# Windowed attention on one core: the first loads issued by GpSimd at once, and the last store split between two queues

## The chip, the cores and the metric

The kernel runs on one core of a Trainium2 chip. The metric is the device time in microseconds (us); the time before is the median of five runs.

## The reference

Attention inside windows of 64 rows, over 4 batches of 4096 rows of 1536 float32 numbers. Every window is on its own.

```
B, S, D = q.shape                      # 4, 4096, 1536, float32
W = 64
q_w = q.reshape(B, S // W, W, D)       # k_w, v_w alike
logits = einsum('bnwd,bnud->bnwu', q_w, k_w) * D ** -0.5
attn = exp(logits - logits.max(-1)) ; attn = attn / attn.sum(-1)
out = einsum('bnwu,bnud->bnwd', attn, v_w)
```

Inputs are three tensors of 100.7 MB each in float32, the output is one more.

## The kernel before, in words

The 16,384 rows are cut into 32 units of 512 rows (UR = 128 x 4 slots; N = 32). For one unit, q, k and v are each 3.15 MB of float32 in HBM and half of that in SBUF, because GpSimd's loads cast to float16 in flight (`load`, line 106). A unit goes through these steps:

- **Transposes** (line 145): TensorE transposes q and k in blocks, two float16 numbers packed as one float32. VectorE and ScalarE copy the results out of PSUM by turns (line 220) into `xq` and `xk`.
- **Products** (line 157): TensorE multiplies the transposed q and k; ScalarE takes the exponential of the four 32x128 blocks that a window pair needs (line 262).
- **Sums and outputs** (line 113): TensorE multiplies by a column of ones for the sums and by v for the outputs. VectorE and ScalarE scale them (lines 249 and 273) into one of three float32 buffers, `outs`.

Loads land in two buffers for each of q, k and v. `hand_over` on GpSimd waits for a landing, waits until the working tile is free, copies it there (line 294), tells TensorE, and requests the load of the unit two ahead into the emptied buffer. So from the start on some six loads and one or two stores are queued in GpSimd's DMA queue, in one fixed order written out by hand: q, k, store of the unit before, v. `store` issues a unit's output as one transfer (line 279). Loads and stores from GpSimd run in one DMA queue, those from SyncE in another; both feed the same 16 DMA engines.

Two places lie outside this pattern.

**The start** (lines 304 to 328). The first q does not come through GpSimd. SyncE loads it as float32 into `outs[0]` in four pieces: two halves of slot 0, slot 1, slots 2 and 3, each with its own semaphore (`d_r0` to `d_r3`). GpSimd waits for the first piece, makes the identity matrix (`affine_select`, line 315), issues the first k and v, and then casts the four slots one by one into `q16` (line 324), waiting for the pieces; between and after the casts it requests the loads of units 1 and 2. SyncE, after its four issues, waits for the identity, the memsets, the four casts, the first k and the first v (lines 353 to 358), and passes these on to TensorE.

**The end** (lines 373 to 390). The last unit's output is stored in two halves, both by SyncE (line 377): the first when each of VectorE and ScalarE has written its first output of the second half, the second when each has written its last. GpSimd drains and raises `done`; SyncE waits for `done` and for all stores (line 387), and clears the semaphores.

Of the kernel before, what the change touches and what calls it, by code (L numbers as in the profile page):

```python
# [17 lines left out]
def kernel(  # L18
# [13 lines left out]
    nc = tc.nc  # L32
    PE, DVE, ACT = (getattr(mybir.EngineType, e) for e in ("PE", "DVE", "Activation"))
    B, S, D = q.shape
    DC = D // (2 * P)
    NJ = D // 512
    SLOTS, R, H = 4, 2, 2
# [3 lines left out]
    qf, kf, vf, of = (x.rearrange("b s d -> (b s) d") for x in (q, k, v, out))  # L41

    def sb(name, shape, dtype):
        return ctx.enter_context(nc.sbuf_tensor(name, shape, dtype))
# [6 lines left out]
    def sem(name):  # L51
        sems.append(nc.alloc_semaphore(name))
        return sems[-1]

    q16 = sb("q16", [P, SLOTS, D], FP16)
    k16 = sb("k16", [P, SLOTS, D], FP16)
# [6 lines left out]
    outs = [sb(f"out{i}", [P, SLOTS, D], FP32) for i in range(NO)]  # L63
# [7 lines left out]
    ops = [ps(f"o{j}", [P, 512]) for j in range(NJ)]  # L71
    sp = ps("sp", [P, 4])

    d_r0, d_r1, d_r2, d_r3, d_k0, d_v0 = (
        sem(n) for n in ("d_r0", "d_r1", "d_r2", "d_r3", "d_k0", "d_v0")
    )
    landed = {x: [sem(f"d_{x}{i + 1}") for i in range(NL)] for x in "qkv"}
    d_o = [sem(f"d_o{i}") for i in range(NO)]
    d_l = [sem(f"d_l{i}") for i in range(2)]
    g_q, g_k, g_v = (sem(n) for n in ("g_q", "g_k", "g_v"))  # L80
# [10 lines left out]
    n_e = [sem("n_ed"), sem("n_ea")]  # L91
    i_d, i_p, c_q, c_l, done = (sem(n) for n in ("i_d", "i_p", "c_q", "c_l", "done"))
# [4 lines left out]
    def rows(x, row0, n, r):  # L97
        return x[row0 : row0 + P * n].rearrange("(h p r) d -> p h (r d)", p=P, r=r)

    def slots(t, lo, hi, r):  # L100
        return t[:, lo:hi, :].rearrange("p (h r) d -> p h (r d)", r=r)

    def load(name, u, dst, s):
        src = {"q": qf, "k": kf, "v": vf}[name]
        r = R if name == "v" else SLOTS
        nc.gpsimd.dma_start(
            out=slots(dst, 0, SLOTS, r), in_=rows(src, u * UR, SLOTS, r)
        ).then_inc(s, 16)
# [169 lines left out]
    def store(u):  # L278
        nc.gpsimd.dma_start(
            out=rows(of, u * UR, SLOTS, R), in_=slots(outs[u % NO], 0, SLOTS, R)  # L280
        ).then_inc(d_o[u % NO], 16)

    def request(x, u):
        if u < N:
            load(x, u, landing[x][u % NL], landed[x][u % NL])
# [3 lines left out]
    def hand_over(x, u, dst, m, g):  # L289

        gp = nc.gpsimd
        gp.wait_ge(landed[x][u % NL], 16 * ((u + u % NL) // NL))
        gp.wait_ge(m, u)
        gp.tensor_copy(  # L294
            out=dst[:, :, :].bitcast(FP32), in_=landing[x][u % NL][:, :, :].bitcast(FP32)
        ).then_inc(c_l, 1)
        copies[0] += 1
        gp.wait_ge(c_l, copies[0])
        gp.sem_inc(g, 1)
        request(x, u + NL)  # L300

    with tc.tile_critical(no_gpsimd_drain=True):

        raw = rows(qf, 0, SLOTS, SLOTS).rearrange("p h (r d) -> p (h r) d", d=D)
        for lo, hi, c0, c1, s in (
            (0, 1, 0, D // 2, d_r0), (0, 1, D // 2, D, d_r1), (1, 2, 0, D, d_r2), (2, SLOTS, 0, D, d_r3)
        ):
            nc.sync.dma_start(
                out=outs[0][:, lo:hi, c0:c1], in_=raw[:, lo:hi, c0:c1]
            ).then_inc(s, 16)  # L310
        nc.vector.memset(ident[:, :], 0.0).then_inc(i_d, 1)
        nc.gpsimd.wait_ge(i_d, 1)

        nc.gpsimd.wait_ge(d_r0, 16)
        nc.gpsimd.affine_select(
            out=ident[:, :], in_=ident[:, :], compare_op=mybir.AluOpType.not_equal,
            fill=1.0, base=0, pattern=[[-1, P]], channel_multiplier=1,
        ).then_inc(i_p, 1)
        load("k", 0, k16, d_k0)
        load("v", 0, v16, d_v0)  # L320

        for i in range(SLOTS):
            nc.gpsimd.wait_ge((d_r1, d_r2, d_r3, d_r3)[i], 16)
            nc.gpsimd.tensor_copy(out=q16[:, i, :], in_=outs[0][:, i, :]).then_inc(c_q, 1)
            if i == 1:
                request("q", 1)
        for x, u in (("k", 1), ("v", 1), ("q", 2), ("k", 2), ("v", 2)):
            request(x, u)

        nc.vector.memset(ones[:, :], 1.0).then_inc(i_d, 1)  # L330
        nc.vector.memset(zeros[:, :], 0.0).then_inc(i_d, 1)
        for et in ets:
            nc.vector.memset(et[:, :, :, :], 0.0).then_inc(i_d, 1)
        nc.scalar.wait_ge(i_d, 5)
        nc.scalar.activation(zeros[:, 3:4], zeros[:, 0:1], EXP, bias=zeros[:, 0:1], scale=1.0)

        with nc.Fori(0, N, engines=OrderedEngineSet([PE]), head_slot={PE: 0}):
            tensor_unit()
        assert N % NO == 2
        for eng, unit in ((DVE, vector_unit), (ACT, scalar_unit)):  # L340
            with nc.Fori(0, N // NO, engines=OrderedEngineSet([eng]), head_slot={eng: 0}):
                for u in range(NO):
                    unit(u)
            for u in range(N - 2, N):
                unit(u)

        sy = nc.sync
        for j in range(NJ):
            for n in (2, 3):
                sy.sem_inc(f_o[j][n], 1)  # L350
        for a in range(2):
            sy.sem_inc(fr[a], NO)
        sy.wait_ge(i_p, 1)
        sy.wait_ge(i_d, 5)
        sy.wait_ge(c_q, SLOTS)
        sy.sem_inc(g_q, 1)
        sy.sem_inc(g_k, 1)._wait_ge(d_k0, 16)
        sy.sem_inc(g_v, 1)._wait_ge(d_v0, 16)
        for u in range(NO, N):
            sy.wait_ge(d_o[u % NO], 16 * (u // NO))  # L360
            for a in range(2):
                sy.sem_inc(fr[a], 1)

        gp = nc.gpsimd
        for u in range(1, N):
            hand_over("q", u, q16, m_q, g_q)
            hand_over("k", u, k16, m_k, g_k)
            gp.wait_ge(m_q, u + 1)
            store(u - 1)
            hand_over("v", u, v16, m_v, g_v)  # L370


        base, o = (N - 1) * UR, outs[(N - 1) % NO]
        for h, c in enumerate((1, 3)):
            for a in range(2):
                sy.wait_ge(n_e[a], c)
            sy.dma_start(
                out=rows(of, base + R * P * h, R, R), in_=slots(o, R * h, R * h + R, R)
            ).then_inc(d_l[h], 16)
        gp.drain()  # L380
        gp.sem_inc(done, 1)
        sy.wait_ge(done, 1)
        for i in range(NO):
            last = max(u for u in range(N - 1) if u % NO == i)
            sy.wait_ge(d_o[i], 16 * (last // NO + 1))
        for i in range(2):
            sy.wait_ge(d_l[i], 16)
        lo, hi = min(s.num for s in sems), max(s.num for s in sems)
        assert hi - lo + 1 == len(sems)
        sy.sem_clear(range(lo, hi + 1))  # L390


# [28 lines left out]
```

## Time and profile before

| what | value |
|---|---|
| median of 5 runs | 942.98 us (942.55 to 943.0) |
| profiled execution, its own time | 942.71 us |
| its span, first to last instruction | 940.9 us |
| its mean granted TensorE clock | 0.857 |
| TensorE busy | 659.4 us (70%) |
| GpSimd busy | 340.4 us (36%) |
| HBM traffic | 301.99 MB read, 100.66 MB written |
| from issue to landing, first k and first v | 12.8 us, 19.4 us |
| from issue to landing, the two last halves (median) | 9.6 us |

The span is the time between the first and the last instruction of one profiled execution; the execution's own time has 1.81 us more around it. In the lines of the profile, "POOL" is GpSimd, "SP" is SyncE, "DVE" VectorE, "ACT" ScalarE and "PE" TensorE. "L106" is line 106 of the kernel; the line of a helper stands for all its calls, so the tile names tell them apart (`q` is q16, `ql` a landing buffer, `out` one of `outs`). A row of the order of time gives start, duration, engine, line, operation, and in brackets the idle time before it with what ended it. A row of the stretches gives the window, its length, the busy time and count of each engine, the granted clock, the mean busy share of the 16 DMA engines and the GB/s they moved, counted on the SBUF side. That share can pass 1, since a transfer's packet is counted whole where it starts. HBM traffic counts float32 bytes, so a cast load counts twice its SBUF bytes there.

### The profile page before, as it was taken

The numbers are of one execution on the slowest core, as the hardware profiler recorded it, in microseconds if no ns is written. First come the engines' busy times: TensorE is split into PE (matmuls) and PEld (weight loads), VectorE is DVE, ScalarE is ACT, GpSimd is POOL, SyncE is SP. The second block draws the span as 40 slices with busy tenths as digits, with TensorE's granted clock in tenths as the row PEclk, the third lists the DMA queues.
The fourth block names the chain that finished last, engine by engine and source line by source line (L and its number), as shares of the span: only waits on it lengthen the run. The fifth ranks groups of instructions, "written<-read, shape, count | busy, mean of one in ns | idle before, by whom it ended". The sixth has DMA issues, their size and how long they took to land. (4 is left out here: it accounts for less than half of the span.)

```text
span 940.9 us, 11422 instructions
## 1 busy us (share of the span) xinstructions
PE 659.4 (70%) x4096; PEld 399.4 (42%) x3456; DVE 279.6 (30%) x453; ACT 335.9 (36%) x642; POOL 340.4 (36%) x228
## 2 busy tenths in 40 slices
PE   1888676866867767677677676776867767677672
PEld 1555344533445334444344543444433355344440
DVE  0433321333313333133332233322333223332231
ACT  1444433333333333332433324333333333343332
POOL 4344333344333443333423334233343333433221
PEclk9999988889888888887988778978888888888887
DMA  9999999999999999999999999999999999999998
GB/s 254 218 215 280 258 243 282 282 282 265 236 281 282 282 275 234 274 282 281 280 235 269 283 280 282 242 261 281 282 282 249 253 281 282 281 258 245 281 300 363
DMA packets 27084, 253.35 MB, mean 269 GB/s; under 512 B 2112, under 2 KB 2112, under 8 KB 10688
## 3 DMA queue, kind: packets, MB, share of 16 engines
q0 software_dynamic: 26208, 246.95, 100.0%
q1 hardware_dynamic: 864, 6.29, 1.7%
q14 instruction: 10, 0.08, 0.0%
q8 instruction: 2, 0.03, 0.0%
HBM read 301.99 MB, written 100.66 MB: 428 GB/s over the span
## 5 line engine op out<-in xcount | busy, mean ns | idle before, releaser
L157 PE MATMUL lt<-xq,xk 128*128 128x256 f16 x1536 | 217.5, 294 | 0.0
L145 PE MATMUL tp<-ident,k 128*128 128x128 f32 x768 | 149.8, 340 | 84.5 <-PEq L211 74.8
L294 POOL COPY v<-vl 128x3072 f32<-128x3072 f32 x31 | 85.2, 2747 | 295.9 <-DMA vl<-in_v_dram 295.9
L157 PEld LDWEIGHTS lt<-xq,xk 128*128 128x128 f16 x1536 | 160.6, 105 | 34.0
L145 PE MATMUL tp<-ident,q 128*128 128x128 f32 x768 | 113.1, 295 | 70.6 <-DVE xq L220 35.3
L145 PEld LDWEIGHTS tp<-ident,k 128*128 128x128 f32 x768 | 115.9, 177 | 104.4 <-issue 101.8
L220 ACT COPY xk<-tp 128x512 f32<-128x512 f32 x96 | 59.5, 620 | 266.1 <-ACTq L211 266.1
L186 PEld LDWEIGHTS <-et 128*128 128x128 f16 x384 | 34.4, 107 | 277.5 <-issue 271.6
L145 PEld LDWEIGHTS tp<-ident,q 128*128 128x128 f32 x768 | 91.8, 151 | 111.4 <-issue 110.8
L220 DVE COPY xk<-tp 128x512 f32<-128x512 f32 x96 | 66.5, 693 | 231.8 <-DVEq L211 231.8
L294 POOL COPY q<-ql 128x3072 f32<-128x3072 f32 x31 | 85.0, 2742 | 110.0 <-DMA ql<-in_q_dram 110.0
L294 POOL COPY k<-kl 128x3072 f32<-128x3072 f32 x31 | 85.2, 2747 | 107.9 <-DMA kl<-in_k_dram 107.9
L113 PE MATMUL o<-v,et 128*128 128x512 f16 x384 | 113.1, 439 | 0.0
L262 ACT ACTIVATE et<-lt,zeros 32x128 f16<-32x128 f32 x256 | 92.1, 360 | 39.4 <-ACTq L211 36.2
L113 PE MATMUL sp<-ones,et 128*128 128x1 f16 x256 | 25.6, 169 | 113.1 <-PEq L211 110.8
L220 ACT COPY xq<-tp 128x512 f32<-128x512 f32 x96 | 59.9, 624 | 125.0 <-ACTq L211 125.0
L249 DVE TENSOR_SCALAR out<-o,rs 128x512 f32<-128x512 f32 x128 | 91.0, 747 | 32.5 <-DVEq L211 28.3
L220 DVE COPY xq<-tp 128x512 f32<-128x512 f32 x96 | 66.3, 690 | 92.6 <-DVEq L211 92.3
L273 ACT ACTIVATE out<-tp,rs 128x512 f32<-128x512 f32 x64 | 44.0, 688 | 135.5 <-ACTq L211 105.0
L113 PE MATMUL tp<-v,et 128*128 128x512 f16 x256 | 91.0, 442 | 0.0
L239 DVE RECIPROCAL rs<-sp 128x2 f32<-128x2 f32 x64 | 10.7, 168 | 260.7 <-DVEq L211 260.6
L113 PE MATMUL lt<-v,et 128*128 128x512 f16 x128 | 57.5, 449 | 0.0
(21 smaller groups left out, 224.0 us busy)
## 6 DMA issues: line engine op xcount, KB each, us to landing
out_dram<-out POOLq DMA_DIRECT2D x31, 3072.0 KB, 61.8
ql<-in_q_dram POOLq DMA_DIRECT2D x31, 1536.0 KB, 54.9
kl<-in_k_dram POOLq DMA_DIRECT2D x31, 1536.0 KB, 54.9
vl<-in_v_dram POOLq DMA_DIRECT2D x31, 1536.0 KB, 54.9
out_dram<-out SPq DMA_DIRECT2D x2, 1536.0 KB, 9.6
out<-in_q_dram SPq DMA_DIRECT2D x1, 1536.0 KB, 13.2
k<-in_k_dram POOLq DMA_DIRECT2D x1, 1536.0 KB, 12.8
v<-in_v_dram POOLq DMA_DIRECT2D x1, 1536.0 KB, 19.4
```

Source lines behind the costliest of these rows:

```text
L113: return nc.tensor.add_instruction(mybir.InstMatmult(name=nc.get_next_instruction_name(), engine=PE, ins=[low(rhs), low(w)], outs=[low(o)] ...
L145: ins = nc.tensor.transpose(tps[g % 2][:, r, j, :], pairs[:, c * P : (c + 1) * P], ident[:, :])
L157: ins = nc.tensor.matmul(lts[h][:, r, :, :], lhsT=halves(xk, c)[:, r, h, :, w], rhs=halves(xq, c)[:, :, h, :, w], start=(c == 0 and w == 0 ...
L186: ld = nc.tensor.ldweights(w)
L220: copy(out=dst, in_=tps[g % 2][:, :, :, :]).then_inc(f_c[g % 4], 1)
L239: ve.reciprocal(out=rs[:, n : n + R], in_=sp[:, n : n + R]).then_inc(n_d, 1)
L249: ins = ve.tensor_scalar_mul(scaled(u, n, j), bank(n, j), scalar1=rs[:, n : n + 1])
L262: ins = sc.activation(ets[h][s, :, :, s], lts[h][s, :, :, s], EXP, bias=zeros[s, 0:1], scale=scale)
L273: ins = sc.activation(scaled(u, n, j), bank(n, j), COPY, bias=0.0, scale=rs[:, n : n + 1])
L294: gp.tensor_copy(out=dst[:, :, :].bitcast(FP32), in_=landing[x][u % NL][:, :, :].bitcast(FP32)).then_inc(c_l, 1)
```

## The change

It has two parts.

- **The start.** SyncE loads only slot 0 of the first q as float32, in one transfer of 0.79 MB, on `d_r0`. GpSimd loads slots 1 to 3 itself, cast to float16, straight into `q16` (a new semaphore, `d_q0`), then the first k; then it makes the identity as soon as the memset is done, loads the first v, and requests all of units 1 and 2. Only then does it wait for `d_r0` and cast the one slot. The other three waits and casts are gone. SyncE waits for one cast and for `d_q0`.
- **The end.** The first half of the last store is issued by GpSimd, the second still by SyncE; each engine waits for the outputs itself. SyncE waits for all stores and raises `done`; GpSimd waits for that and clears the semaphores.

```diff
-        raw = rows(qf, 0, SLOTS, SLOTS).rearrange("p h (r d) -> p (h r) d", d=D)
-        for lo, hi, c0, c1, s in (
-            (0, 1, 0, D // 2, d_r0), (0, 1, D // 2, D, d_r1), (1, 2, 0, D, d_r2), (2, SLOTS, 0, D, d_r3)
-        ):
-            nc.sync.dma_start(
-                out=outs[0][:, lo:hi, c0:c1], in_=raw[:, lo:hi, c0:c1]
-            ).then_inc(s, 16)
+        first = rows(qf, 0, SLOTS, SLOTS)
+        nc.sync.dma_start(out=outs[0][:, 0, :], in_=first[:, 0, :D]).then_inc(d_r0, 16)
+        nc.gpsimd.dma_start(
+            out=q16[:, 1:, :].rearrange("p r d -> p (r d)"), in_=first[:, 0, D:]
+        ).then_inc(d_q0, 16)
+        load("k", 0, k16, d_k0)
         nc.vector.memset(ident[:, :], 0.0).then_inc(i_d, 1)
         nc.gpsimd.wait_ge(i_d, 1)
-
-        nc.gpsimd.wait_ge(d_r0, 16)
         nc.gpsimd.affine_select(
...
-        load("k", 0, k16, d_k0)
         load("v", 0, v16, d_v0)
-
-        for i in range(SLOTS):
-            nc.gpsimd.wait_ge((d_r1, d_r2, d_r3, d_r3)[i], 16)
-            nc.gpsimd.tensor_copy(out=q16[:, i, :], in_=outs[0][:, i, :]).then_inc(c_q, 1)
-            if i == 1:
-                request("q", 1)
-        for x, u in (("k", 1), ("v", 1), ("q", 2), ("k", 2), ("v", 2)):
-            request(x, u)
+        for u in (1, 2):
+            for x in "qkv":
+                request(x, u)
+        nc.gpsimd.wait_ge(d_r0, 16)
+        nc.gpsimd.tensor_copy(out=q16[:, 0, :], in_=outs[0][:, 0, :]).then_inc(c_q, 1)
...
-        sy.wait_ge(c_q, SLOTS)
-        sy.sem_inc(g_q, 1)
+        sy.wait_ge(c_q, 1)
+        sy.sem_inc(g_q, 1)._wait_ge(d_q0, 16)
...
-        for h, c in enumerate((1, 3)):
+        for h, (eng, c) in enumerate(((gp, 1), (sy, 3))):
             for a in range(2):
-                sy.wait_ge(n_e[a], c)
-            sy.dma_start(
+                eng.wait_ge(n_e[a], c)
+            eng.dma_start(
...
         gp.drain()
-        gp.sem_inc(done, 1)
-        sy.wait_ge(done, 1)
         for i in range(NO):
...
+        sy.sem_inc(done, 1)
+        gp.wait_ge(done, 1)
...
-        sy.sem_clear(range(lo, hi + 1))
+        gp.sem_clear(range(lo, hi + 1))
```

More of the change, by code (lines that the diff above doesn't have):

```diff
@@ L72 @@
     sp = ps("sp", [P, 4])
-    d_r0, d_r1, d_r2, d_r3, d_k0, d_v0 = (
-        sem(n) for n in ("d_r0", "d_r1", "d_r2", "d_r3", "d_k0", "d_v0")
-    )
+    d_r0, d_q0, d_k0, d_v0 = (sem(n) for n in ("d_r0", "d_q0", "d_k0", "d_v0"))
     landed = {x: [sem(f"d_{x}{i + 1}") for i in range(NL)] for x in "qkv"}
```

## The prediction

> **What bounds the kernel now.** I read the page's slices first, then the DMA queues, then the stretches of the start and the end, GpSimd's order of time over the first 25 us, SyncE's waits, and last the trace's single DMA records.
>
> ```profile
> span 940.9 us, 11422 instructions
> PE 659.4 (70%) x4096; PEld 399.4 (42%) x3456; DVE 279.6 (30%) x453; ACT 335.9 (36%) x642; POOL 340.4 (36%) x228
> DMA  9999999999999999999999999999999999999998
> HBM read 301.99 MB, written 100.66 MB: 428 GB/s over the span
> ```
>
> No engine is over 70% busy, and the DMA row is full in every slice but the last. The kernel moves 402.65 MB and is done when they are moved. Where, then, are the DMA engines not full?
>
> ```profile
> 0.00:2.00 2.00, 0.00 (x0) 0.00 (x0) 0.74 (x5) 1.09 (x1) 0.20 (x4) 1.00 0.01 3
> 2.00:12.00 10.00, 0.00 (x0) 0.00 (x0) 0.00 (x0) 0.49 (x2) 4.99 (x6) 1.00 1.03 352
> ...
> 928.00:936.50 8.50, 0.00 (x0) 0.00 (x0) 0.71 (x2) 0.30 (x1) 0.00 (x0) 0.64 1.01 430
> 936.50:939.00 2.50, 0.00 (x0) 0.00 (x0) 0.00 (x0) 0.00 (x0) 0.00 (x0) 0.50 0.31 133
> 939.00:940.90 1.90, 0.00 (x0) 0.00 (x0) 0.00 (x0) 0.00 (x0) 0.00 (x0) 0.50 0.00 0
> ```
>
> The last two columns are the DMA engines' busy share and GB/s. Only two places are open: the first 2.0 us, and the end, where the share falls to 0.31 from 936.5 on. There the 16 engines finish at different times. The single records say how: each transfer leaves 16 completion marks, one for each engine. Those of the last transfer lie at 936.94 to 937.31 for ten engines and at 938.58, 938.83, 938.93, 939.00, 939.58 and 939.62 for six. The hindmost mark is 2.0 to 2.9 us behind the main group in nearly every transfer since the first, so I take it for one engine throughout. That engine sets the end: after the first k (its mark at 20.06) it does 126 further transfers of 3.15 MB of float32 in 919.56 us, 7.30 each, never waiting.
>
> SyncE's waits agree: its last wait is for DMA (line 387), not for an engine. The next view is GpSimd's order of time.
>
> ```profile
> 6.77 0.28 POOL L315 TENSOR_SCALAR_AFFINE_SELECT ident<-ident 128x128 f32<-128x128 f32 x1 [6.32 <-DMA out<-in_q_dram]
> 7.29 0.68 POOL L106 DMA_DIRECT2D k<-in_k_dram  x1 [0.25 <-issue]
> 7.97 0.72 POOL L106 DMA_DIRECT2D v<-in_v_dram  x1
> 8.67 2.90 POOL L324 CAST q<-out 128x1536 f16<-128x1536 f32 x2
> ...
> 15.63 2.87 POOL L324 CAST q<-out 128x1536 f16<-128x1536 f32 x2 [3.56 <-DMA out<-in_q_dram]
> ```
>
> GpSimd idles for 6.3 us and starts k at 7.29. It looks like lost time, but the stretch 2 to 12 shows the DMA engines at 1.03 under it.
>
> **The change, part by part.**
>
> *Waits and casts at the start.* Gone: the wait of 6.3 us for the first SyncE load, the later one of 3.56, and three of the four casts (3 x 1.48 = 4.4 us of GpSimd). Nine GpSimd issues (0.55 to 0.75 each) now stand from about 0.95, an estimate from SyncE's own first issue at 0.96, to about 7.3; behind them wait only the identity's place among them (the memset it needs ends at 1.2), the one cast (1.48) and the hand-over of unit 1, whose q does not land before 34.67. TensorE starts earlier than 18.9, at about 13. But k lands at 17.9 to 20.06 in either case, v at 27.4, and unit 1's q at 34.67, because the DMA order q, k, v, q1, k1, v1, q2, k2, v2 is the same. Worth: 0. The cover is the DMA queue; were it empty, the 6.3 us would show in full.
>
> *Bytes.* HBM still gives 3.15 MB of q. Three quarters now come cast in the DMA. On one DMA engine, marks of the hindmost lie 7.34 us apart from k to v (12,288 B of float32 a packet), 7.27 from v to q1 (24,576 B), and a float32 store has 16 packets of 0.457 = 7.31. All three are the same price for a byte of float32; the new packet (18,432 B) lies between. So 0.0, bounds -0.1 and +0.1.
>
> *A hole between the two queues.* SyncE's single load holds as many bytes as its first two before; their later marks lie at 4.52 to 5.24 on 14 engines, less some 0.34 from packet to mark: 4.2 to 4.9. GpSimd's k was issued at 7.29 and its first packet ran at 10.29, so a GpSimd load takes at most 3.0 us to its first packet. Issued at 0.95 that is 3.95 at the latest, before the quarter is done. Hole: 0. Below zero nothing is to be had, since SyncE's first packet stands at 1.97, 1.0 us after an issue that does not move.
>
> *The hindmost engine's start lag.* Up to its mark at 20.06 it has its first packet at 2.17, two transfers' worth (14.6) and 3.3 of something else. The records show what: a first packet of 1.26 us instead of 0.12, and code fetches of 0.755 and 1.08 us at 3.54 and 4.33. 1.14 + 1.84 = 2.98. Does the change move these? The fetches of the compute engines cannot move; GpSimd's and SyncE's own can. Two more fetches of 0.45 us ran at 9.06 and 9.27, which would add 0.9 if they fell on this engine. If instead the lag vanished, the gain would be the distance to the next engine at the end, 2.53 - 1.91 = 0.6, because four others have gathered 1.5 to 1.9 us by the end, three of them largely in the steady run. I take 0, nearest to an unchanged set of fetches; bounds -0.6 and +0.9.
>
> *The last store.* Its first half goes from SyncE (0.35 us to issue, 1.0 to the first packet) to GpSimd, which is idle from 920.5 on: 0.71 to issue, at most 3.0 to the first packet. Issued at 927.6, it can run from 930.6. What covers it: store 30 ahead in GpSimd's queue, and the second half from SyncE at 929.7. On the main group store 30 runs out at about 929.0, a hole of up to 0.7 us on engines with 2.5 to spare. The hindmost, some 5 packets behind, has store 30 until about 931.6. Cost 0; the cover gone, it would be 2.0.
>
> [...] Beside VectorE's PSUM reads the 31 GpSimd stores took 704 to 716 ns to issue, without one slow case. [...]
>
> *The end's hand-off.* Before, SyncE passed its last wait at the last mark and cleared the semaphores itself. Now it raises "done", GpSimd waits for it and clears. GpSimd's drain comes earlier and is covered by 11 us of DMA. One hop more: between SyncE's own semaphore step (0.03) and the longest wait between engines in the exit (0.4); I take 0.1, near its usual steps.
>
> The sum: profiled run 942.71 (span 940.9 and 1.81 around it) + 0.0 + 0.0 + 0.0 + 0.1 = 942.8. The median of the runs shown is 0.27 above that run, so 943.1.
>
> **Rivals.**
>
> *Slower: GpSimd's first load comes late.* Place: the DMA engines after SyncE's quarter. For it: so early an issue is not in this trace, with nine queued on end and memsets beside them. Against: the 3.0 us above, which already contains a first use. Price: the hindmost engine is busy until 2.17 + 1.14 + 1.84 + 1.85 = 7.0, and the others have 2.5 us to spare after about 4.4; so from a first packet at 6.9 each further us costs one. It passes 0.2% (1.9 us) from 8.8, 7.9 us after the issue. At 10 it gives 946.2.
>
> *Faster: the start packs better.* With four SyncE loads merged and the fetches spread, the hindmost engine loses its lag (0.6) and the main group part of its own. That group's marks for k lie near 18.1, which is 2.0 + 14.6 + 0.34 and 1.1 more; if both go and the drifters of the steady run go with them, at most 0.6 + 1.1 = 1.7 by these rows, 941.4. Over 1.9 needs the steady drift to shrink too, of which I see no cause.
>
> *A new bound at the end: the late half.* GpSimd's half starting after 931.6 would leave even the hindmost engine dry, at one us for each us. SyncE's half, 8 packets of 0.46 on each engine, covers it to about 935.3. It gives at most a few tenths, 943.4.
>
> *It does nothing it says:* the start is freed on GpSimd and not in the DMA; that is my forecast itself.
>
> **How the numbers follow.** No difference beyond 0.2%, about what a measurement of this kernel can tell from no change: 0.68, taking in the forecast, the late half and small start shifts (941.2 to 944.9). Slower by more: 0.20, of it 0.12 for the late first load and 0.08 for fetches and stalls piling onto the hindmost engine, the one cost that the trace bounds poorly. Faster by more: 0.12, for a better packed start together with a drift I did not foresee. The forecast's own range from the bounds is 943.1 - 0.6 - 0.1 to 943.1 + 0.9 + 0.1 + 0.3 (the hand-off at 0.4), or 942.4 to 944.4. To leave out no more than 2 in 10 it is widened into both rivals: 941.0 to 945.6.
>
> **What would show it.** Right: the DMA row full from 2.0 to 936 again, the first TensorE transposes at about 13 instead of 18.9, k's last mark near 20, the end falling off over some 2.5 us with ten engines together, and SyncE's last wait for DMA. Wrong: a stretch under 0.9 between 3 and 9 us (the late load), a last k mark off 20 by more than 1 us (the lag moved), or a share under 0.9 between 929 and 936 (the late half). If the marks of the main group and the hindmost lie elsewhere but the time holds, it is right for a wrong reason.

## The result, and the profile after

The changed kernel takes 945.15 us (median of 22 runs, 943.94 to 945.52); the kernel before, beside it, 942.95 (42 runs). The ratio is 1.0022, 95% interval 1.0016 to 1.0028: 2.2 us slower, 2.05 above the forecast of 943.1.

The page of the changed kernel, its head, TensorE's row, the DMA row of the slices and the HBM line:

```profile
span 943.4 us, 11416 instructions
PE 659.0 (70%) x4096; PEld 401.8 (43%) x3456; DVE 279.6 (30%) x453; ACT 334.7 (35%) x642; POOL 337.8 (36%) x227
DMA  9999999999999999999999999999999999999997
HBM read 301.99 MB, written 100.66 MB: 427 GB/s over the span
```

Same bytes, same engines, and still a 9 in every slice but the last. That row cannot place the loss: a slice is 23.6 us, a 9 is anything from 90% on, and 2.2 us are 9% of one slice. The stretches say where it is; the last two columns are the DMA engines' busy share and GB/s.

```profile
0.00:2.00 2.00, 0.00 (x0) 0.00 (x0) 0.73 (x5) 1.09 (x1) 0.72 (x5) 1.00 0.06 12
2.00:12.00 10.00, 0.00 (x0) 0.00 (x0) 0.00 (x0) 0.49 (x2) 6.71 (x11) 1.00 1.04 241
...
928.00:936.50 8.50, 0.00 (x0) 0.00 (x0) 0.00 (x0) 0.00 (x0) 0.00 (x0) 0.60 1.02 434
936.50:939.00 2.50, 0.00 (x0) 0.00 (x0) 0.00 (x0) 0.00 (x0) 0.00 (x0) 0.50 0.30 128
939.00:940.90 1.90, 0.00 (x0) 0.00 (x0) 0.00 (x0) 0.00 (x0) 0.00 (x0) 0.50 0.00 0
940.90:943.40 2.50, 0.00 (x0) 0.00 (x0) 0.00 (x0) 0.00 (x0) 0.00 (x0) 0.50 0.01 3
```

The DMA engines start and stop as before: 1.04 under the start, 0.30 in the 2.5 us in which they finish one after another, nothing after 939.0. (The 3 GB/s in the last row are one code fetch at 940.94.) New is the last row, 2.5 us in which no compute engine works and the DMA engines move nothing but that. The span is longer by just that. What is waited for there stands among SyncE's waits (engine, line, releaser: us in total, times, longest), first of the kernel before, then of the changed one:

```profile
SPq L387 <- DMA out_dram<-out: 10.4, 2, 6.8
```

```profile
SPq L376 <- DMA out_dram<-out: 11.9, 1, 11.9
SPq L300 <- POOLq L300: 1.9, 1, 1.9
```

Before, the wait for DMA was the last long one. Now one for GpSimd follows it (line 300, where at the end of the program the engines wait for one another). And GpSimd, which by its busy time does nothing, is inside its `drain`; the clear behind it in the program starts only when that has ended. The page leaves drains out of busy time, so one has to ask for their line: 380 before, 371 in the changed kernel (count, shortest, median and longest in ns, first and last start in us).

```profile
L380 POOLq DRAIN  x1: 14972/14972/14972, 920.6 to 920.6; - x1
```

```profile
L371 POOLq DRAIN  x1: 15611/15611/15611, 926.5 to 926.5; - x1
```

Both last some 15 us. Before, it ran from 920.58 to 935.55 and so ended four microseconds before SyncE's last two stores had landed. In the changed kernel it runs from 926.50 to 942.11. The single records give the rest: the last completion mark of all stands at 939.77 (before: 939.62), SyncE raises `done` at 940.29, and GpSimd begins to clear the semaphores at 942.15, 0.04 after its drain. From the last mark to the clear it is 2.38 us instead of 0.08; from the clear to the end 1.20 instead of 1.22. So 0.15 + 2.30 - 0.02 = 2.43, and the profiled executions differ by 945.13 - 942.71 = 2.42.

What does the drain wait for? Not for all DMA: before, it was over 4.1 us ahead of SyncE's last mark. In both traces it ends 2.3 us after the last mark of the last transfer that *GpSimd itself* had issued: store 30, the output of the last unit but one, before (933.25 to 935.55, 2.30), its half of the last store now (939.77 to 942.11, 2.34).

### The profile page after: what moved, and what is told of

Same layout as the page of the kernel before. It is cut to its first block, busy times and chain, and to the rows that moved or that the text cites. A ratio compares the mean times of both kernels' runs of the same rounds, so it can differ in the third digit from the quotient of the medians.

```text
span 943.4 us, 11416 instructions
## 1 busy us (share of the span) xinstructions
PE 659.0 (70%) x4096; PEld 401.8 (43%) x3456; DVE 279.6 (30%) x453; ACT 334.7 (35%) x642; POOL 337.8 (36%) x227
## 5 line engine op out<-in xcount | busy, mean ns | idle before, releaser
L155 PE MATMUL lt<-xq,xk 128*128 128x256 f16 x1536 | 220.2, 297 | 0.0
L111 PE MATMUL o<-v,et 128*128 128x512 f16 x384 | 109.7, 429 | 0.0
L111 PE MATMUL tp<-v,et 128*128 128x512 f16 x256 | 89.1, 434 | 0.0
L247 DVE TENSOR_SCALAR out<-tp,rs 128x512 f32<-128x512 f32 x64 | 48.0, 751 | 29.8 <-DVEq L209 29.8
```

Of the source, the lines that this page charges most:

```text
L111: return nc.tensor.add_instruction(mybir.InstMatmult(name=nc.get_next_instruction_name(), engine=PE, ins=[low(rhs), low(w)], outs=[low(o)] ...
L155: ins = nc.tensor.matmul(lts[h][:, r, :, :], lhsT=halves(xk, c)[:, r, h, :, w], rhs=halves(xq, c)[:, :, h, :, w], start=(c == 0 and w == 0 ...
L247: ins = ve.tensor_scalar_mul(scaled(u, n, j), bank(n, j), scalar1=rs[:, n : n + 1])
```

## The experiments

Theory A: GpSimd's drain ends a fixed 2.3 us after the last mark of GpSimd's own last transfer, and since the change that is the last thing to end. The rivals are that the start costs (B), that the clearing handed to GpSimd costs (C), that splitting the last store over two queues costs (D).

**One part each.** e1 has the new start and the old end, e2 the old start and the new end; the edit is the diff of the change, cut between the two parts at the line `base, o = ...`.

> The start of the changed kernel with the end of the kernel before. Theory A (the whole loss is GpSimd's drain at the end, which lasts until some 2.3 us after the last mark of GpSimd's own last store): the drain is then covered again, 943.0 us, between 942.5 and 943.4, drain over by about 935.7. Theory B (the start costs, the hindmost DMA engine has more lag): 944.8 to 945.3, drain covered all the same.

> The start of the kernel before with the end of the changed one. Theory A: 945.1 us, between 944.7 and 945.5, GpSimd's drain over 2.3 us after the last completion mark. Theory B: 943.0 to 943.3.

Measured: e1 943.19 us, ratio to before 1.0005 (0.9996 to 1.0014); e2 944.85, ratio 1.0025 (1.0015 to 1.0034). The drain's line in each, and the wait that it causes in e2:

```profile
L371 POOLq DRAIN  x1: 16742/16742/16742, 921.1 to 921.1; - x1
```

```profile
L380 POOLq DRAIN  x1: 13647/13647/13647, 927.2 to 927.2; - x1
SPq L302 <- POOLq L302: 1.8, 1, 1.8
```

The end alone loses what the whole change loses, and the start makes no measurable difference: the upper end of e1's interval is 1.3 us, less than the loss. B is out as its cause.

**The order of closing, with the half store kept on GpSimd** (e3), **and without it** (e4).

```diff
 e3, to the changed kernel
         gp.drain()
+        gp.sem_inc(done, 1)
+        sy.wait_ge(done, 1)
...
-        sy.sem_inc(done, 1)
-        gp.wait_ge(done, 1)
-        gp.sem_clear(range(lo, hi + 1))
+        sy.sem_clear(range(lo, hi + 1))

 e4, to the changed kernel
-        for h, (eng, c) in enumerate(((gp, 1), (sy, 3))):
+        for h, c in enumerate((1, 3)):
             for a in range(2):
-                eng.wait_ge(n_e[a], c)
-            eng.dma_start(
+                sy.wait_ge(n_e[a], c)
+            sy.dma_start(
```

> The changed kernel with GpSimd's half store and drain kept, but the closing order of before: GpSimd raises done after its drain, SyncE waits for it and clears. Theory A: the drain still ends last, 944.9 us, between 944.4 and 945.3. Theory C (the cost is the clearing handed to GpSimd, with its wait and its clear of 0.33 us): 943.0 to 943.3.

> The changed kernel with both half stores on SyncE as before, and the clearing still handed to GpSimd. Theory A: the drain follows store 30 alone and is over by about 935.7; what is left is the hand-off, 943.3 us, between 942.8 and 943.6. Theory C: 944.7 to 945.3.

Measured: e3 945.33, ratio 1.0026 (1.0016 to 1.0035), a little over the upper end that theory A gave; e4 942.89, ratio 1.0002 (0.9993 to 1.0011). Who clears does not matter. In e4, with the clear on GpSimd, the profile goes from SyncE's signal at 939.83 to the clear at 939.88: the hand-off that I had priced at 0.1 costs 0.05. In e3, with the clear on SyncE, the wait is there all the same and names the drain's line:

```profile
SPq L381 <- POOLq L371: 2.0, 1, 2.0
```

C is out. e4 also shows the drain when store 30 is again GpSimd's last transfer:

```profile
L371 POOLq DRAIN  x1: 16732/16732/16732, 920.7 to 920.7; - x1
```

It is over at 937.48 (in e1 at 937.83), and the last mark of all is at 939.74: covered. Both are some 2 us later than the 935.7 that I expected, because store 30's own last mark came at 935.18 and 935.53 there, not at 933.25; the 2.30 after it held.

**Another second queue** (e5), **less behind the drain** (e6), **more behind it** (e7).

```diff
 e5, to the changed kernel (the line is cut on both sides)
     -  enumerate(((gp, 1), (sy, 3)))
     +  enumerate(((nc.scalar, 1), (sy, 3)))

 e6, for the first half (in short; SyncE's part has a semaphore of its own, which SyncE waits for)
     -  gp: out=rows(of, base, R, R), in_=slots(o, 0, R, R)
     +  gp: out=rows(of, base, R, R)[:, :, D:], in_=slots(o, 0, R, R)[:, :, D:]
     +  sy: out=rows(of, base, R, R)[:, :, :D], in_=slots(o, 0, R, R)[:, :, :D]

 e7, to the changed kernel
     -  enumerate(((gp, 1), (sy, 3)))
     +  enumerate(((gp, 1), (gp, 3)))
```

> The changed kernel with the first half of the last store issued by ScalarE instead of GpSimd, still another queue than SyncE's; GpSimd drains after store 30 and clears as in the changed kernel. Theory A (GpSimd's drain ends 2.30 to 2.35 us after the last mark of GpSimd's own last transfer and is what ends last): 943.0 us, between 942.6 and 943.5, drain over before 938. Theory D (splitting the last store over two queues is what costs, because the halves end together): 944.8 to 945.4.

> The changed kernel with GpSimd storing only slot 1 of the last unit (a quarter of it, 0.79 MB) and SyncE slot 0 and the second half. Theory A: GpSimd's last mark moves ahead by about 1 us, to some 938.6, the drain ends at 940.9 and shows by 1.2 us instead of 2.3: 944.1 us, between 943.5 and 944.6, drain end minus last GpSimd mark again 2.30 to 2.35. Theory D: 944.8 to 945.4, as in the changed kernel.

> The changed kernel with both halves of the last store issued by GpSimd: twice the bytes behind the drain. Theory A: the drain cannot begin to end later than the last mark of all plus 2.3, so the cost does not double: 945.2 us, between 944.8 and 945.7. A theory that the drain's price grows with what GpSimd stores at the end: 947.

Measured: e5 943.45, ratio 1.0007 (0.9998 to 1.0016); e6 943.85, ratio 1.0012 (1.0003 to 1.0021); e7 945.17, ratio 1.0027 (1.0016 to 1.0037). Two queues, SyncE's and ScalarE's, are no measurable loss, so D is out (e5's interval ends at 944.5, below the 944.8 that D asks for). A quarter on GpSimd loses less, by the ratios about half as much (0.0012 against 0.0022), though the interval of e6 is too wide to say how much; twice the bytes lose no more. In e6 the profiled execution (944.48) lies above its median: GpSimd's last mark came at 939.09 there, not at the 938.6 that I had worked out. The drain's line in e5:

```profile
L371 POOLq DRAIN  x1: 18110/18110/18110, 920.5 to 920.5; - x1
```

The waits and the drain's line in e6:

```profile
SPq L301 <- POOLq L301: 1.5, 1, 1.5
```

```profile
L379 POOLq DRAIN  x1: 12212/12212/12212, 929.2 to 929.2; - x1
```

and the drain's line in e7, where it starts latest of all and still does not end before 942.06:

```profile
L371 POOLq DRAIN  x1: 12678/12678/12678, 929.4 to 929.4; - x1
```

All profiles together, read from their single records (us from the span's start; "own time" is the profiled execution's):

| kernel | last mark of GpSimd's last transfer | drain ends | after it by | last mark of all | own time | median |
|---|---|---|---|---|---|---|
| before | 933.25 | 935.55 | 2.30 | 939.62 | 942.71 | 942.95 |
| changed | 939.77 | 942.11 | 2.34 | 939.77 | 945.13 | 945.15 |
| e1, start only | 935.53 | 937.83 | 2.30 | 940.09 | 943.19 | 943.19 |
| e2, end only | 938.55 | 940.90 | 2.35 | 939.15 | 943.94 | 944.85 |
| e3, SyncE clears | 939.46 | 941.80 | 2.34 | 939.92 | 944.84 | 945.33 |
| e4, halves on SyncE | 935.18 | 937.48 | 2.30 | 939.74 | 942.86 | 942.89 |
| e5, half on ScalarE | 936.32 | 938.62 | 2.30 | 939.70 | 943.19 | 943.45 |
| e6, quarter on GpSimd | 939.09 | 941.43 | 2.34 | 939.94 | 944.48 | 943.85 |
| e7, both on GpSimd | 939.68 | 942.06 | 2.38 | 939.68 | 945.09 | 945.17 |

The fourth column is the same within 0.08 us in all nine, whatever the drain's start (920.5 to 929.4) and whatever GpSimd stores last (0.79, 1.57 or 3.15 MB). And the own time is, in eight of nine, the later of "drain ends" and "last mark of all" plus 3.02 to 3.12 us. In e2, whose profiled execution is the shortest of its ten, the two go together: it is 1.2 us shorter than the changed kernel's, and its drain ends 1.2 us sooner. The ninth is e5, with 3.49: 0.44 of it is a gap between SyncE's last two waits (939.71 to 940.15). The changed kernel has the same gap, 939.85 to 940.29, there under the drain; so has e7 (939.89 to 940.33), and e4 has none. In the three traces with the gap the last code fetch on the DMA engines starts 0.65 us after it (940.80, 940.94 and 940.98); in before, e1, e2, e4 and e6 the last code fetch is at 930.5 to 933.0, and SyncE shows no such gap; in e3 SyncE's wait for the drain lies where it would show. The two go together, but that one makes the other is not shown.

Not tried: the changed kernel without its drain. What the drain waits for was moved instead. No version beat the kernel before: the nearest, e4, lies at 1.0002 with 1 inside its interval.

## Why the prediction was right or wrong

**The time: inside the range, and by luck.** 945.15 lies in the stated 941.0 to 945.6, but outside the 942.4 to 944.4 that the prediction worked out from its own bounds. The upper part had been added for a late first load and for stalls on the hindmost DMA engine, and neither occurred. The outcome to which the prediction gave the most, no difference beyond 0.2%, is not what the median shows (1.0022, with 1.002 inside its interval); slower had 0.20, for those same two reasons.

**The end's hand-off: wrong, and it accounts for the error.** The step reads "GpSimd's drain comes earlier and is covered by 11 us of DMA", and the term was 0.1. The hand-off itself measures 0.05 (e4). The drain does begin well ahead of the end (at 926.50, later than the 920.58 of before, with 13 us of DMA still to run), but it ends 2.3 us after GpSimd's own last transfer, and the same change put that transfer last of all. The cover of 11 us was real and of no use, since what covers and what is waited for are the same DMA. The term is 2.3 us. The row that held the price was in the trace of before, 14,972 ns at line 380: a drain that ends 2.30 us after a mark, under a cover of 4.1 us (935.55 to 939.62). The prediction does not use it.

**The last store: half right.** The DMA engines as a group did not run dry (a mean share of 1.02 from 928 to 936.5), and the late half did not decide (its last mark is 0.15 behind the last mark of before). But I priced moving the half only to its first packet and did not follow its completion: who waits for GpSimd's own last transfer? No issue of GpSimd was slow in the changed kernel: the half store took 0.56 us (at 926.52), beside VectorE's last outputs, which read PSUM; the nine issues at the start took 0.55 to 0.76, the first of them 0.66 with memsets of VectorE beside it; the 31 whole stores took 0.71 to 0.72. (In the trace of before, VectorE was at work beside 29 of the 31 stores, not beside all.)

**The start: right, in size and step by step.** e1 gives 1.0005 with 1 inside the interval. The steps hold one by one in the changed kernel's GpSimd rows, in order of time:

```profile
1.48 0.66 POOL L304 DMA_DIRECT2D q<-in_q_dram  x1 [1.04 <-SPq L300]
2.14 0.56 POOL L104 DMA_DIRECT2D k<-in_k_dram  x1
...
6.55 0.76 POOL L104 DMA_DIRECT2D vl<-in_v_dram  x1
7.26 1.53 POOL L319 CAST q<-out 128x1536 f16<-128x1536 f32 x1
```

GpSimd starts at 1.48, not at the 0.95 that I estimated, and its first packet runs at 4.30, 2.8 us later, inside the bound of 3.0; SyncE's quarter is done between 4.3 and 4.85 on 14 DMA engines and at 6.0 and 6.4 on two, so no hole shows. TensorE's first transpose is at 12.57 (forecast 13, before 18.9). Those 6.3 us gained on TensorE are worth nothing, as k still lands when the DMA order lets it: its last mark is at 19.55, before at 20.06.

**The hindmost DMA engine: right in kind, small in size.** It gained 0.5 at k and had lost it again by the end: its last marks, 939.77 and 939.62, differ by 0.15. The bounds of -0.6 and +0.9 hold. That it is one engine throughout remains an inference; the records carry no engine number. Nor do they say whose a code fetch is, so that the compute engines' fetches cannot move was my assumption: the five of the start began at 3.76, 4.08, 4.57, 10.05 and 10.06, before at 3.54, 4.33, 4.41, 9.06 and 9.27.

**The rivals.** Slower came out, but for a reason that none of them named. The late first load did not occur. The better packed start did not show beyond the 0.5. Of the signs of being right, the last failed: SyncE's last long wait is for GpSimd (1.9 us at line 300), not for DMA. The signs of being wrong all lay before the last mark, none in the stretch after it.

## What to carry to other kernels

GpSimd's drain at the end lasted here, in nine profiles, until 2.30 to 2.38 us after the last mark of GpSimd's own last transfer. So when a transfer is moved to another engine's queue, look for a drain on that engine and add its tail (here 2.3 us) to the transfer's last mark. Instructions that a page does not count as busy must be asked for by their line; one that is hidden by 4 us in the trace of before is a cost in waiting. Where one resource is full from end to end, as the DMA engines are here, freeing engines at the start brought nothing (e1, 1.0005), and what can still be lost lies ahead of its first packet and behind its last mark.

## What the runs showed of the hardware that was not expected

GpSimd's drain ends 2.30 to 2.38 us after the last completion mark of GpSimd's own last DMA transfer, in nine profiles (the table has each), and does not wait for transfers of SyncE or ScalarE (in e5 it is over at 938.62, with their last mark at 939.70). The transfers' own semaphores are there earlier: SyncE passes its wait for the same transfer 0.01 us after that mark in the changed kernel (939.77 to 939.78). Where the 2.3 us go inside the drain, no view of the profile shows.
